# Where the weights lie against the moving tiles: other gaps in SBUF in a two-level Strassen-like short-convolution layer

## The chip, the cores and the metric

The kernel runs on one core of one Trainium2 chip. The metric is device microseconds from launch to end, the median of several runs. The kernel before took 771.57 us (3 runs, 770.79 to 771.90).

## What is computed

With DEPTH = 1 only layer 0 of the reference runs, so the whole computation is one gated short-convolution mixer between two RMS norms, in float32:

```python
u = rms_norm(x, pre_norm)                       # x: 1024 frames x 1024
z, bg, cg, v = split(u @ w_in, 4)               # w_in: 1024 x 8192, four parts of 2048
y = bg * causal_dwconv(cg * v, conv_w) * silu(z)   # 3 taps along the frames
out = x + rms_norm(y @ w_out, post_norm)        # w_out: 2048 x 1024
```

## The kernel before, in words

**Products.** Both matrix products are done in seven products a to g instead of eight (Strassen's scheme in Winograd's form, over halves of the frames and of the contraction). An operand is a sum of blocks, split into a high and a low part in the format fp32r; each product of two blocks is three matmuls, low by high, high by low, high by high. `product` (main stage) issues for one of the 32 pairs of weight rows and one letter 4 x 3 matmuls of 128 by 128 weights with 512 moving columns. For most of the chunks, the products b, f and g are in turn done in seven products a' to g' (`deep_product`): 2 x 3 matmuls each with 256 moving columns. b is done so in 14 chunks, f in 13 and g in 12; elsewhere b, f and g are 512 columns wide like a, c, d, e. The output stage has `out_mm` (512 columns, letters a, c, e, d, g) and `small_mm` (256 columns, for b and f).

**Operands in SBUF.** In the main stage the *moving* operand is a tile U of one letter (`u_a` to `u_g`, 16 KB in each partition) or a second-level sum of parts of it (`ub..`, `uf..`, `ug.._deep`, 2 KB each, in the pool `tmp`). The *weights* lie in pages of 2 KB (`wah`, `wal`, `dwb0h` ...). The weight load of the next matmul runs while the present matmul streams its columns. In the output stage both operands of a product lie in the seven slots that held the U tiles: `ou_*`, `oB*`, `ox_*` move, `oy_*`, `oA*`, `ox_*` are weights. Every slice that a matmul takes begins a multiple of 512 bytes behind its tile's start, so that the distance from the moving operand to the weights, modulo 512, is the same for all matmuls of one pair of tiles. This text calls it **d**: address of the weights less address of the moving operand, modulo 512.

**What sets the addresses.** SBUF pools are laid one behind another in the order in which they are opened. `Shelves` opens one pool for each group of slots in `U_LAYOUT` (the first number names the slots, the second the bytes left free behind the group, by `gap`); `U_SLOTS` says in which slot each tile comes to lie (a: 5, b: 4, c: 2, e: 6, d: 1, f: 3, and g: 0 after the input tile `xb`). Then come 32 pages, then the gap `room_tmp`, then the head's tiles (`xa`, gone after the head) and in their place the pool `tmp` with the second-level sums.

```python
for n, (slots, room) in enumerate(U_LAYOUT):
    pool = ctx.enter_context(tc.tile_pool(name=f"up{n}", bufs=1))
    self.at.update({s: pool for s in slots})
    gap(ctx, tc, f"room{n}", room)
```

The tiles that the pools give out have these places, modulo 512:

| tiles | before |
|---|---|
| U of b, f, g (slots 4, 3, 0) | 64 |
| U of a, c, d, e (slots 5, 2, 1, 6) | 128 |
| pages (all weights of the main stage, all loads) | 128 |
| second-level sums | 64 |
| `xa`, later `gpad` and `acc` | 32 |

So d is 0 for a, c, d and e, and 64 for b, f, g and the second level. In the output stage d is 0, 64 or 448 (that is, -64), by the slots of the two operands.

**Order of the work.** A planner (`Plan`) records the program, sorts each engine's instructions by due times from the table `PLAN`, and emits them. All matmuls come in the order in which they were recorded.

Of the kernel before, what the change touches and what calls it, by code (L numbers as in the profile page):

```python
# [199 lines left out]
class Op:  # L200
# [2 lines left out]


U_LAYOUT = (
    ((0,3,4,), 64),
    ((1,2,5,6,), 0),
)
U_SLOTS = (5, 4, 2, 6, 1, 3, 0, 0, 5, 2, 6, 4, 1, 3, 0, 5, 2, 6, 4, 1, 6, 3, 0, 4, 2, 5, 6, 1, 0, 3, 2, 4, 5, 6, 0, 4, 1, 5, 3, 6, 0, 2)
# [2 lines left out]
def gap(ctx, tc, name, size):  # L212

    if size:
        ctx.enter_context(tc.tile_pool(name=name, bufs=1)).tile([128, size // 4], F32, tag=name, name=name)
# [426 lines left out]
def kernel(  # L642
# [365 lines left out]

    mixed = ExitStack()
    head = ExitStack()  # L1010
    gap(ctx, tc, "room_tmp", 416)
    hp = plan.pool(head.enter_context(tc.tile_pool(name="head", bufs=1, reuse_waits="tile")), 1)

    xa = hp.tile([P, TH, D], F32, tag="xa", name="xa")
# [1079 lines left out]
```

## Time and profile before

| | |
|---|---|
| median of 3 runs | 771.57 us |
| the profiled execution's own time | 771.06 us |
| its span, first to last instruction | 769.3 us |
| TensorE (PE) | 759.3 us busy, 4320 matmuls |
| weight loads (PEld) | 666.1 us, 4320 |
| VectorE (DVE) | 679.9 us |
| ScalarE (ACT) | 459.1 us |
| GpSimd (POOL) | 464.3 us |
| granted clock of TensorE | 0.998 |

The profiled execution's own time is 1.8 us over its span, which is what lies outside the first and last instruction. A matmul's row in the timeline has its start and its modelled length; since matmuls overlap in the pipeline, the time that one costs is read from the start of one row to the start of the next, which this text calls the **pitch**. Rows of the timeline merge neighbours of the same tiles (x2, x24, x96).

### The profile page before, as it was taken

The numbers are of one execution on the slowest core, as the hardware profiler recorded it, in microseconds if no ns is written. First come the engines' busy times: TensorE is split into PE (matmuls) and PEld (weight loads), VectorE is DVE, ScalarE is ACT, GpSimd is POOL, SyncE is SP. The second block draws the span as 40 slices with busy tenths as digits, with TensorE's granted clock in tenths as the row PEclk, the third lists the DMA queues.
The fourth block names the chain that finished last, engine by engine and source line by source line (L and its number), as shares of the span: only waits on it lengthen the run. The fifth ranks groups of instructions, "written<-read, shape, count | busy, mean of one in ns | idle before, by whom it ended". The sixth has DMA issues, their size and how long they took to land.

```text
span 769.3 us, 12814 instructions
## 1 busy us (share of the span) xinstructions
PE 759.3 (99%) x4320; PEld 666.1 (87%) x4320; DVE 679.9 (88%) x1022; ACT 459.1 (60%) x880; POOL 464.3 (60%) x416
## 2 busy tenths in 40 slices
PE   8999999999999999999999999999999999999996
PEld 7888889898989898988898998989888889889885
DVE  6899978999888989999989999799998898877993
ACT  7765678675656565556555665556653656565731
POOL 2509997889675778696789678585639100700421
PEclk9999999999999999999999999999999999999999
DMA  9212425344333547566858484927465998566842
GB/s 316 69 53 71 123 79 150 105 128 141 100 117 97 171 111 198 137 177 174 239 138 240 110 234 107 251 84 217 127 174 177 332 373 289 199 220 205 276 149 109
DMA packets 117137, 130.11 MB, mean 169 GB/s; under 512 B 7320, under 2 KB 74704, under 8 KB 116944
## 3 DMA queue, kind: packets, MB, share of 16 engines
q1 hardware_dynamic: 112560, 120.77, 49.2%
q0 software_dynamic: 4352, 8.39, 7.0%
q8 instruction: 34, 0.56, 0.3%
q14 instruction: 31, 0.25, 0.1%
q10 hardware_dynamic: 160, 0.14, 0.1%
HBM read 101.74 MB, written 44.30 MB: 190 GB/s over the span
## 4 chain that ended last, share of the span: by engine, by line
PE 98%; DVE 1%; DMA 0%; ACT 0%; POOL 0%; issue 0%; POOLq 0%; ACTq 0%
PE px L279 39%; PE pv L279 15%; PE po_x L279 11%; PE px2b L279 5%; PE px2f L279 4%; PE px2g L279 3%; PE pp L279 3%; PE po_v L279 3%; PE pv2b L279 3%; PE pv2f L279 2%; PE pf_x L279 1%; PE pb_x L279 1%; PE py2b L279 1%; PE py L279 1%; PE pv2g L279 1%; PE pb_v L279 1%
## 5 line engine op out<-in xcount | busy, mean ns | idle before, releaser
L279 PE MATMUL px<-u_c,wch 128*128 128x512 f32 x248 | 76.5, 389 | 0.0
L279 PE MATMUL px<-u_a,wah 128*128 128x512 f32 x248 | 76.4, 389 | 0.0
L279 PE MATMUL px<-u_d,wdh 128*128 128x512 f32 x248 | 76.4, 389 | 0.0
L279 PE MATMUL pv<-u_e,weh 128*128 128x512 f32 x248 | 76.4, 389 | 0.0
L279 ACT COPY beside<-raw 128x512 f32<-128x512 f32 x67 | 39.6, 591 | 31.9 <-DVE dwf2l L279 10.5
L279 DVE SCALAR_TENSOR_TENSOR cv<-gpad,cw,cv 128x1024 f32<-128x1024 f32 x32 | 51.7, 1615 | 2.9 <-ACT cv L279 2.6
L279 PEld LDWEIGHTS px<-u_c,wch 128*128 128x128 f32 x248 | 46.6, 188 | 8.8
L279 PEld LDWEIGHTS px<-u_a,wah 128*128 128x128 f32 x248 | 46.5, 188 | 8.7
L279 PEld LDWEIGHTS pv<-u_e,weh 128*128 128x128 f32 x248 | 46.6, 188 | 8.7
L279 PEld LDWEIGHTS px<-u_d,wdh 128*128 128x128 f32 x248 | 46.5, 188 | 8.6
L279 POOL TENSOR_TENSOR sf<-raw,sc 128x512 f32<-128x512 f32 x30 | 46.4, 1545 | 10.1 <-DVE sc L279 5.8
L279 PE MATMUL px<-u_d,wdl 128*128 128x512 f32 x124 | 48.4, 390 | 0.0
L279 PE MATMUL px<-u_a,wal 128*128 128x512 f32 x124 | 48.3, 390 | 0.0
L279 PE MATMUL px<-u_c,wcl 128*128 128x512 f32 x124 | 48.3, 389 | 0.0
L279 PE MATMUL pv<-u_e,wel 128*128 128x512 f32 x124 | 48.2, 389 | 0.0
L279 POOL TENSOR_TENSOR rs_post<-ve_post,minus_half 128x1 f32<-128x1 f32 x7 | 6.5, 942 | 67.6 <-DVE ve_post L279 67.6
L279 POOL TENSOR_TENSOR raw<-raw,raw 128x512 f32<-128x512 f32 x31 | 44.6, 1437 | 3.3 <-DVE se L279 1.9
L279 POOL TENSOR_TENSOR sc<-se,raw 128x512 f32<-128x512 f32 x25 | 35.1, 1404 | 18.5 <-PE px2b L279 7.9
L279 ACT COPY sna<-px 128x512 f32<-128x512 f32 x30 | 17.6, 585 | 45.5 <-PE px L279 45.5
L279 POOL TENSOR_TENSOR se<-raw,raw 128x512 f32<-128x512 f32 x22 | 33.0, 1500 | 16.7 <-DMA raw<-in_sc_w_in 11.1
L279 DVE TENSOR_TENSOR wcl<-sc,wch 128x512 fp32r<-128x512 f32 x31 | 31.6, 1018 | 3.5 <-ACT wch L279 3.5
L279 POOL TENSOR_TENSOR sne<-snc,sne 128x512 f32<-128x512 f32 x12 | 18.4, 1536 | 23.1 <-ACT snc L279 23.1
(486 smaller groups left out, 2643.5 us busy)
## 6 DMA issues: line engine op xcount, KB each, us to landing
raw<-in_sc_w_in SPq DMA_DIRECT2D x128, 256.0 KB, 4.3
y_d<-cv SPq DMA_DIRECT2D x16, 512.0 KB, 2.9
s_d<-s SPq DMA_DIRECT2D x32, 256.0 KB, 4.7
t_d<-in_sc_w_out POOLq DMA_DIRECT2D x16, 512.0 KB, 8.8
tb<-in_sc_w_out SPq DMA_DIRECT2D x16, 256.0 KB, 3.2
t_d<-in_sc_w_out SPq DMA_DIRECT2D x16, 256.0 KB, 4.7
t_d<-t_d SPq DMA_DIRECT2D x16, 256.0 KB, 4.5
s<-y_d SPq DMA_DIRECT2D x16, 256.0 KB, 4.5
```

The lines of the kernel that those rows point to most:

```text
L279: getattr(engine, name)(*(self.plain(a) for a in args), **{k: self.plain(a) for k, a in kw.items()})
```

## The change

It changes free bytes between tiles, and nothing else: the group of slots 0, 3, 4 becomes three groups, with 64, 64 and 96 free bytes behind them, and the gap `room_tmp` shrinks from 416 to 192 bytes.

```diff
 U_LAYOUT = (
-    ((0,3,4,), 64),
+    ((0,), 64),
+    ((3,), 64),
+    ((4,), 96),
     ((1,2,5,6,), 0),
 )
...
-    gap(ctx, tc, "room_tmp", 416)
+    gap(ctx, tc, "room_tmp", 192)
```

Every engine has the same instructions in the same order with the same waits before and after; only the addresses differ. They become, modulo 512:

| tiles | before | after | d before | d after |
|---|---|---|---|---|
| U of b (slot 4) | 64 | 192 | 64 | 96 |
| U of f (slot 3) | 64 | 128 | 64 | 160 |
| U of g (slot 0) | 64 | 64 | 64 | 224 |
| second-level sums | 64 | 0 | 64 | 288 |
| U of a, c, d, e (slots 5, 2, 1, 6) | 128 | 288 | 0 | 0 |
| pages | 128 | 288 | | |
| `xa`, `gpad`, `acc` | 32 | 480 | | |

In the output stage, by weights and moving operand:

| products | matmuls | d before | d after |
|---|---|---|---|
| `oy`,`ou` of a0, c0, e1, d1 | 4 x 48, 512 columns | 0 | 0 |
| c1; d0 | 48; 48 | 0 | 64; 128 |
| a1, e0; g0; g1 | 96; 48; 48 | 448 | 416; 352; 288 |
| `oA1_b`,`oB1_b` | 24, 256 columns | 448 | 288 |
| `ox_b`,`oB2_b`; `oA3_f`,`oB3_f` | 24; 24 | 448 | 416 |
| `oA1_b`,`oB3_b`; `oA3_f`,`oB1_f` | 24; 24 | 0 | 448; 128 |
| `oA3_b`,`oB3_b`; `oA2_f`,`oB2_f`; `ox_f`,`oB2_f` | 3 x 24 | 64 | 160 |
| `oA2_b`,`ox_b` | 24 | 64 | 96 |
| `oA1_f`,`oB1_f` | 24 | 64 | 224 |
| the other four of 256 columns | 4 x 24 | 0 | 0 |

One more thing is different: before, the U tiles, the pages and the second-level sums all begin at a multiple of 64 bytes; after, the U tiles of a, c, d, e and the pages begin 32 bytes past one.

## The prediction

> **What bounds the kernel.** I read the page's first part and its chain first: who is busy all the time, and whose work makes up the chain that ended last.
>
> ```profile
> PE 759.3 (99%) x4320; PEld 666.1 (87%) x4320; DVE 679.9 (88%) x1022; ACT 459.1 (60%) x880; POOL 464.3 (60%) x416
> PE 98%; DVE 1%; DMA 0%; ACT 0%; POOL 0%; issue 0%; POOLq 0%; ACTq 0%
> ```
>
> TensorE is busy for 99% of the span and makes up 98% of the chain. There is next to no wait to take away or to add: the time is the sum of the matmuls' pitches, and a change of addresses can act on it through the pitch alone. So I looked for the pitch by d in the timeline of TensorE, from the start of the first row of a run of matmuls to the start of the next run.
>
> First 512 columns, at d = 0 (`u_c`, 12 matmuls) and at d = 64 (`u_f`, 12 matmuls, starting at 607.17 and ending where `ubgh_deep` begins):
>
> ```profile
> 355.74 0.39 PE L279 MATMUL px<-u_c,wcl 128*128 128x512 f32 x1
> ...
> 358.46 0.28 PE L279 MATMUL px<-uggh_deep,dwg 128*128 128x256 f32 x1
> ...
> 607.17 0.39 PE L279 MATMUL pv<-u_f,wfl 128*128 128x512 f32 x1
> ...
> 609.97 0.28 PE L279 MATMUL px2b<-ubgh_deep,dwb 128*128 128x256 f32 x1
> ```
>
> At d = 0 the twelve take 358.46 - 355.74 = 2.72 us, 226.7 ns each; at d = 64 they take 609.97 - 607.17 = 2.80 us, 233.3 ns each. The granted clock is 0.998 over the whole span (front table), so the clock is not the reason. It isn't an accident of two places either: the groups of all matmuls of a kind show the same in a matmul's length.
>
> ```profile
> L279 PE MATMUL px<-u_c,wch 128*128 128x512 f32 x248 | 76.5, 389 | 0.0
> L279 PE MATMUL px<-u_g,wgh 128*128 128x512 f32 x56 | 17.6, 394 | 0.0
> L279 PE MATMUL pv<-u_f,wfh 128*128 128x512 f32 x40 | 12.5, 394 | 0.0
> L279 PE MATMUL py<-u_b,wbh 128*128 128x512 f32 x24 | 7.5, 394 | 0.0
> L279 PE MATMUL pp<-u_b,wn11h 128*128 128x512 f32 x8 | 2.7, 394 | 0.0
> ```
>
> `u_c` (d = 0) has a mean of 389 ns, `u_g`, `u_f` and `u_b` (d = 64) 394 ns in every group. All three kinds have 128 by 128 weights and 512 columns; what the layout sets apart is d.
>
> Then 256 columns at d = 64 in the main stage, 24 matmuls of `u_b`, `u_f` and two second-level sums in one run up to the next `u_d`:
>
> ```profile
> 379.12 0.28 PE L279 MATMUL pv2b<-u_b,dwb2l 128*128 128x256 f32 x1
> ...
> 381.95 0.39 PE L279 MATMUL px<-u_d,wdl 128*128 128x512 f32 x1
> ```
>
> 381.95 - 379.12 = 2.83 us, 117.9 ns each (117.5 in the twelve rows from 358.46 on); I take **117.7**. The other values of d at 256 columns, and d = 448 at 512, stand in the output stage, where one row merges a whole product:
>
> ```profile
> 613.46 22.05 PE L279 MATMUL po_x<-ou_a,oy_a 128*128 128x512 f32 x96
> 635.34 2.99 PE L279 MATMUL pb_x<-oB_b,oA_b 128*128 128x256 f32 x24
> 638.17 3.03 PE L279 MATMUL pb_y<-oB_b,oA_b 128*128 128x256 f32 x24
> 641.03 2.90 PE L279 MATMUL pb_x<-oB_b,oA_b 128*128 128x256 f32 x24
> 643.77 3.02 PE L279 MATMUL pb_v<-oB_b,oA_b 128*128 128x256 f32 x24
> ...
> 652.32 2.89 PE L279 MATMUL pb_x<-ox_b,oA_b 128*128 128x256 f32 x24
> 655.05 21.95 PE L279 MATMUL po_x<-ou_c,oy_c 128*128 128x512 f32 x96
> 676.83 22.06 PE L279 MATMUL po_v<-ou_e,oy_e 128*128 128x512 f32 x96
> ...
> 698.74 2.99 PE L279 MATMUL pf_x<-oB_f,oA_f 128*128 128x256 f32 x24
> 701.56 2.99 PE L279 MATMUL pf_y<-oB_f,oA_f 128*128 128x256 f32 x24
> ```
>
> A run's time is the next row's start less its own. At d = 448: 638.17 - 635.34 = 2.83, 117.9 ns. At d = 0: 641.03 - 638.17 = 2.86, 119.2 ns. At d = 64 there are two answers: 698.74 to 701.56 is 2.82, **117.5**, but 641.03 to 643.77 is 2.74, 114.2, and 652.32 to 655.05 is 2.73, **113.8**. For 512 columns, `ou_c` (both halves d = 0) takes 676.83 - 655.05 = 21.78 for 96, 226.9 ns; `ou_a` takes 21.88, and with its first half at d = 0 (48 x 0.2269 = 10.89) the second, at d = 448, is left with 10.99, **229.0 ns**.
>
> So the trace has three values of d out of the sixteen multiples of 32. With 512 columns 0 is the best (226.8) and both neighbours are dearer; with 256 columns 0 is the dearest (119.2), and the neighbours cost 117.7 or, in some runs, 114. A matmul's length follows the pitch and names these states:
>
> ```profile
> L279 PE MATMUL pb_y<-oB_b,oA_b 128*128 128x256 f32 x24 | 3.0, 282 | 0.0
> L279 PE MATMUL pb_x<-ox_b,oA_b 128*128 128x256 f32 x24 | 2.9, 276 | 0.0
> L279 PE MATMUL px2b<-u_b,dwb0h x56: 281/281/281, 106.5 to 584.3; 128*128 128x256 f32 x56
> ```
>
> The product at 119.2 has a mean length of 282 ns, the one at 113.8 of 276, and `u_b` in the main stage (the third row: least, median and greatest length, first and last start) 281 from first to last. What it doesn't show is any of the new values 96, 160, 224, 288, 352 and 416.
>
> On this a rule of the Trainium skill speaks against the change. "TensorE: Matmul & The Clock Gate", Part 2, step 1, says that the moving operand and the weight load have two independent SBUF read ports, so that loading the next weights takes no read bandwidth from the running matmul; and "SBUF — State Buffer", section "Who interferes with whom", that TensorE never waits on anyone. By that rule d could not matter; the trace does not agree (226.7 against 233.3 ns above).
>
> **The change part by part.** No instruction, wait or transfer is added, removed or moved past another, so everything is count times pitch.
>
> *The second level, main stage.* The counts come from these groups; a group has 4 matmuls a chunk, which gives 14, 13 and 12 chunks, 39 in all.
>
> ```profile
> L279 PE MATMUL px2b<-u_b,dwb0h 128*128 128x256 f32 x56 | 10.5, 281 | 0.0
> L279 PE MATMUL px2f<-u_f,dwf0h 128*128 128x256 f32 x52 | 9.8, 281 | 0.0
> L279 PE MATMUL px<-u_g,dwg0h 128*128 128x256 f32 x48 | 9.0, 281 | 0.0
> ```
>
> 39 chunks x 7 products x 6 matmuls = 1638 matmuls of 256 columns, all at d = 64 now (336 `u_b`, 312 `u_f`, 288 `u_g`, 702 second-level sums), and at 96, 160, 224 and 288 after. Bounds of a new pitch: 113.8 from below, 119.2 from above, so 1638 x -3.9 = -6.4 us to 1638 x 1.5 = +2.5 us. I take 117.7, no change: it is the main stage's own row at d = 64, and the row at the other side of zero (448) has 117.9; two values of d that are far apart in address agree on it.
>
> *b, f and g of 512 columns.* The groups above hold 56 + 40 + 24 high-weight matmuls; the low weights add half as many, 180 in all, and the first products of `u_b` and `u_f` another 48 (the row of `pp<-u_b` and three like it, 8 high each and half as many low). 228 matmuls, now at 233.3. Bounds: down to 226.7 (-1.5 us); nothing dearer than 233.3 is shown for a steady run, and I let the other end be as far above, +1.5 us, an estimate. I take no change.
>
> *The output stage, 512 columns.* c1 and d0 leave d = 0 for 64 and 128: 96 x (233.3 - 226.7) = +0.6 us, where 64 is a value that the trace has. a1, e0, g0 and g1 leave 448 (229.0) for 416, 352 and 288: 192 matmuls, bounds 226.7 and 233.3, -0.4 to +0.8 us; I take the upper, since with 512 columns every step away from zero costs, and 448 is the one nearest to it: +0.8 us.
>
> *The output stage, 256 columns.* Two products leave d = 0: 48 x (117.7 - 119.2) = -0.1 us. Three of those at d = 64 now run at 114 and leave for 160 and 96; at 117.7 that is 72 x 3.7 = +0.3 us. The rest stays where it is.
>
> *Products that keep d = 0.* 4 x 372 in the main stage (248 + 124, from the `u_c` group) and 4 x 48 in the output stage, 1680 matmuls; their operands move together, now to 32 bytes past a multiple of 64. I take nothing, from tiles that lie so already: `xa` is at 32, `xb` at 64 modulo 512.
>
> ```profile
> L279 PEld LDWEIGHTS pk<-ident,xa x32: 138/140/143, 7.4 to 16.6; 128*128 128x128 f32 x32
> L279 PEld LDWEIGHTS pk<-ident,xb x32: 139/140/143, 26.7 to 38.6; 128*128 128x128 f32 x32
> L279 DVE TENSOR_SCALAR xa<-xa,rs_pre x5: 480/752/753, 6.6 to 11.9; 128x1024 f32<-128x1024 f32 x3, 128x512 f32<-128x512 f32 x2
> L279 DVE TENSOR_SCALAR xb<-xb,rs_second x2: 747/750/753, 24.1 to 24.7; 128x1024 f32<-128x1024 f32 x2
> ```
>
> A weight load from either takes 140 ns, and VectorE 750 to 752 ns. No *moving* operand lies so in the trace, which leaves a case open below. The head's transposes (weights from `xa`, d from 416 to 352) are bound to these loads, and I leave them as they are. "SBUF — State Buffer" in the Trainium skill (the box on cachelines) counts SBUF lines of 16 bytes; all the new addresses are multiples of 32, and by that rule this part costs nothing, as I take it.
>
> **Sum:** 0 + 0 + 0.6 + 0.8 - 0.1 + 0.3 = +1.6 us on the execution's own 771.06, 772.7. The median is 771.57, 0.5 above it, so the median becomes 771.57 + 1.6 = **773.2 us**. It all reaches the end, since TensorE has no gap that could hide it.
>
> **The rivals.** *A, faster: the second level falls into the quick rhythm.* At d = 64 the same matmuls run at 117.7 in one place and at 113.8 in another, steadily each; where the weight load meets the stream at another point, the 1638 may settle at 114. For it: the quick rhythm exists, and 0 is the worst d with 256 columns, so that more distance may be better. Against: in the main stage d = 64 never leaves 281, from 106.5 to 584.3 us. Price -6.4 + 1.6 = -4.8, **766.8 us**; with the 512-column ones at 226.7 too and no loss in the output stage, 771.6 - 6.4 - 1.5 = 763.7. It decides once some 700 of the 1638 (the sums alone) are quick: 702 x -3.9 = -2.7. VectorE would allow it:
>
> ```profile
> 500.00:600.00 100.00, 100.00 (x568) 87.81 (x567) 93.75 (x134) 55.47 (x103) 65.17 (x55) 1.00 0.55 161
> ```
>
> Its 93.75 of 100 us leave 6, and the gain is under 1%.
>
> *B, slower: the second level meets as at d = 0.* If its new places act like 0, 1638 x 1.5 = +2.5, with the rest +4.1: **775.7 us**, more if a place is worse than any shown. For it: three values don't map sixteen. Against: 64 and 448 both avoid it.
>
> *C, slower: a stream that begins 32 bytes past a multiple of 64 costs extra.* Price for 1680 matmuls between the step from 226.8 to 229.0 (2.2 ns, +3.7) and that to 233.3 (6.6 ns, +11.1): 776.9 to 784.3, with the rest; the nearest row gives **776.9**. For it: no moving operand lies so before. Against: loads and VectorE don't care.
>
> *D: the change does nothing,* because d isn't the cause of the rows above: **771.6 us**. Against: the groups at 389 and 394, and the output stage's rows, which differ by slot alone. The rule of the Trainium skill on the two read ports, cited above, would give this time.
>
> **How the numbers follow.** A measurement of this kernel can tell about 0.2%, 1.5 us, from no change. Chances: my forecast 0.36 (its own range 771 to 775, since +0.6 rests on rows and +0.8 on a bound; 0.22 slower, 0.12 within, 0.02 faster), A 0.32 (0.30 faster, 0.02 within), B 0.15, C 0.12, D 0.05. Faster 0.32, within 0.19, slower 0.22 + 0.15 + 0.12 = 0.49. The range takes in A but for its best end and C's lower part: 764.5 to 779; beyond it I leave 0.05 below and 0.09 above.
>
> **What would show it.** In the profile after, the groups of `u_b`, `u_f`, `u_g` and the sums by form give each new d its own pitch: my forecast wants lengths of 281 at 256 columns and 394 at 512. Lengths near 276 in the sums and `u_b` are A, 282 and more are B. `u_c` at 389 denies C, 391 or more shows it. `ou_c` should take 22.1 us for its 96 instead of 21.78. I am wrong if the pitch depends on d in finer steps than the trace shows, and wholly if a group that keeps its d changes.

## The result, and the profile after

| | before | after |
|---|---|---|
| median of 3 runs | 771.57 us (770.79 to 771.90) | 776.75 us (776.65 to 776.80) |
| ratio, 95% interval | | 1.0069 (1.0046 to 1.0092) |
| the profiled execution's span | 769.3 us | 774.9 us |
| granted clock of TensorE | 0.998 | 0.997 |

The change costs 5.2 us, 0.7%, which is slower by more than the 0.2% that can be told here. The prediction had 773.2: slower was its likeliest case, but it took +1.6 where +5.2 came. The page after, busy time of each engine, and its chain by engine:

```profile
PE 765.6 (99%) x4320; PEld 668.5 (86%) x4320; DVE 673.9 (87%) x1022; ACT 458.5 (59%) x880; POOL 461.4 (60%) x416
...
PE 98%; DVE 1%; DMA 0%; ACT 0%; POOL 0%; issue 0%; POOLq 0%; ACTq 0%
```

The shape is as before: TensorE is busy for 99% of the span and is 98% of the chain, with as many matmuls, and its busy time has grown by 765.6 - 759.3 = 6.3 us. (VectorE and GpSimd have become shorter by 6 and 3 us, which nobody waits for.) So the question is which matmuls have a longer pitch. First the output stage after, in rows of the timeline (start, length, and so on as before):

```profile
617.00 22.28 PE L281 MATMUL po_x<-ou_a,oy_a 128*128 128x512 f32 x96
639.12 3.01 PE L281 MATMUL pb_x<-oB_b,oA_b 128*128 128x256 f32 x24
641.96 3.04 PE L281 MATMUL pb_y<-oB_b,oA_b 128*128 128x256 f32 x24
644.84 3.04 PE L281 MATMUL pb_x<-oB_b,oA_b 128*128 128x256 f32 x24
647.72 3.03 PE L281 MATMUL pb_v<-oB_b,oA_b 128*128 128x256 f32 x24
...
656.30 3.01 PE L281 MATMUL pb_x<-ox_b,oA_b 128*128 128x256 f32 x24
659.15 22.26 PE L281 MATMUL po_x<-ou_c,oy_c 128*128 128x512 f32 x96
681.25 22.30 PE L281 MATMUL po_v<-ou_e,oy_e 128*128 128x512 f32 x96
```

`ou_c` takes 681.25 - 659.15 = 22.10 us for its 96 matmuls, the figure that the prediction gave, against 21.78 before. `ou_a` takes 639.12 - 617.00 = 22.12 against 21.88. Of 256 columns, the third row of `pb` (from 644.84: `oA3_b`,`oB3_b`, now at d = 160) takes 647.72 - 644.84 = 2.88 us for its 24, 120.0 ns each, where the same row took 2.74 before; the quick rhythm of 114 ns that it had is gone, and so it is in `ox_b` (659.15 - 656.30 = 2.85, 118.8 ns each, at d = 96).

Then the groups of the main stage after, by form (busy us, mean ns of one, idle before):

```profile
L281 PE MATMUL px<-u_a,wah 128*128 128x512 f32 x248 | 77.1, 392 | 0.0
L281 PE MATMUL pv<-u_e,weh 128*128 128x512 f32 x248 | 77.0, 392 | 0.0
L281 PE MATMUL px<-u_c,wch 128*128 128x512 f32 x248 | 76.8, 391 | 0.0
L281 PE MATMUL px<-u_d,wdh 128*128 128x512 f32 x248 | 76.7, 390 | 0.0
...
L281 PE MATMUL px2b<-u_b,dwb0h 128*128 128x256 f32 x56 | 10.7, 283 | 0.0
L281 PE MATMUL px2f<-u_f,dwf0h 128*128 128x256 f32 x52 | 10.0, 286 | 0.0
L281 PE MATMUL px<-u_g,dwg0h 128*128 128x256 f32 x48 | 9.0, 280 | 0.0
```

The last three are the ones whose d changed: 283, 286 and 280 ns where all had 281. The first four kept d = 0 and were at 389 before (the row of `u_c` in the prediction); now they have 392, 392, 391 and 390. That is the outcome for which the prediction said that it would be wholly wrong.

From all matmul records of the two traces, each pitch (start to next start) summed by class:

| class | matmuls | d before, after | mean pitch before, after (ns) | difference (us) | forecast |
|---|---|---|---|---|---|
| `u_a`, `u_e`, `u_c`, `u_d` | 1536 | 0, 0 | 229.7, 227.3, 227.1, 227.1; 231.7, 229.7, 229.5, 228.1 | 0.78 + 0.92 + 0.87 + 0.36 = **+2.93** | 0 |
| output, 512 columns | 288 | 0 or 448; 64, 128, 288, 352, 416 | 226.9 to 229.4; 233.3 to 233.9 | **+1.47** | +1.4 |
| output, 256 columns | 336 | as in the table of the change | | **+0.53** | +0.2 |
| second level: `u_b` | 336 | 64, 96 | 118.1, 118.8 | +0.23 | 0 |
| second level: `u_f` | 312 | 64, 160 | 118.1, 119.6 | +0.47 | 0 |
| second level: `u_g` | 288 | 64, 224 | 117.8, 117.0 | -0.23 | 0 |
| second level: sums | 702 | 64, 288 | 118.1, 118.2 | +0.08 | 0 |
| `u_b`, `u_f`, `u_g`, 512 columns | 228 | 64; 96, 160, 224 | | +0.15 | 0 |

They add up to 5.63; with the small rest the sum over all records is 5.58, and the span grew by 774.9 - 769.3 = 5.6. More than half of it is in products whose operands lie exactly as far apart as before.

Where inside such a product the time goes is seen in the rows of one run of `u_c` after (a row of one and a row of two make three matmuls):

```profile
374.71 0.39 PE L281 MATMUL px<-u_c,wcl 128*128 128x512 f32 x1
...
375.41 0.40 PE L281 MATMUL px<-u_c,wcl 128*128 128x512 f32 x1
...
376.10 0.39 PE L281 MATMUL px<-u_c,wcl 128*128 128x512 f32 x1
...
376.79 0.39 PE L281 MATMUL px<-u_c,wcl 128*128 128x512 f32 x1
...
377.47 0.28 PE L281 MATMUL px2f<-ufch_deep,dwf1l 128*128 128x256 f32 x1
```

The run of 12 takes 377.47 - 374.71 = 2.76 us, not 2.72; each third of it has 0.70, 0.69, 0.69 and 0.68 us. It starts slow and comes to the old pitch (0.68 for three, 226.7 each) at its end. The single pitches of such runs, as medians by position in the trace, in ns:

```
u_c after u_g at 224: 234 229 231 231 236 228 233 231 226 227 227 226   2759 in all, 12 runs
u_e after sums at 288: 233 236 228 233 231 227 227 226 227 227 226 227   2747, 12 runs
u_e after u_f at 160: 233 233 236 224 231 236 228 233 231 226 227 227   2764, 13 runs
u_e before, after 256 columns at 64: 227 throughout                     2720, 25 runs
```

In the first and the third row the product ahead is six matmuls long, and six sums at 288 stand ahead of it.

### The profile page after: what moved, and what is told of

It is laid out like the page before. It is cut to its first block, busy times and chain, and to the rows that moved or that the text cites. A ratio compares the mean times of both kernels' runs of the same rounds, so it can differ in the third digit from the quotient of the medians.

```text
span 774.9 us, 12814 instructions
## 1 busy us (share of the span) xinstructions
PE 765.6 (99%) x4320; PEld 668.5 (86%) x4320; DVE 673.9 (87%) x1022; ACT 458.5 (59%) x880; POOL 461.4 (60%) x416
## 4 chain that ended last, share of the span: by engine, by line
PE 98%; DVE 1%; DMA 0%; ACT 0%; POOL 0%; issue 0%; POOLq 0%; ACTq 0%
PE px L281 39%; PE pv L281 15%; PE po_x L281 11%; PE px2b L281 5%; PE px2f L281 4%; PE px2g L281 3%; PE pp L281 3%; PE po_v L281 3%; PE pv2b L281 3%; PE pv2f L281 2%; PE pf_x L281 1%; PE pb_x L281 1%; PE py2b L281 1%; PE py L281 1%; PE pv2g L281 1%; PE pb_v L281 1%
## 5 line engine op out<-in xcount | busy, mean ns | idle before, releaser
L281 POOL TENSOR_TENSOR sf<-raw,sc 128x512 f32<-128x512 f32 x30 | 44.8, 1495 | 11.1 <-DVE sc L281 5.9
L281 DVE TENSOR_TENSOR sna<-px2b,sna 128x256 f32<-128x256 f32 x56 | 23.1, 413 | 11.8 <-PE px2b L281 11.8
```

The source lines that it names most:

```text
L281: getattr(engine, name)(*(self.plain(a) for a in args), **{k: self.plain(a) for k, a in kw.items()})
```

## The experiments

**The theories.** *T, carried over:* the matmuls of a run at d = 0 settle at 226.7 ns only after some that are slower, and how many those are is set by the product that ran just before; after second-level matmuls at d = 64 there are none, after the new distances the list of single pitches has 3 to 9 ahead of the first 227. Worked out for `u_e`: 13 runs x 44 ns + 12 x 27 = 0.90 us, of +0.92 measured. Over all four letters, the 103 runs of twelve that stand behind 256 columns take 3.17 us more than 103 x 2720 ns after the change and 0.35 more before it (pauses of single matmuls): 2.82 of the +2.93. *C, the prediction's rival:* a moving operand that begins 32 bytes past a multiple of 64 costs extra. Already against C: in the output stage after, `ou` of a0, c0, e1 and d1 lie so as well, and have 226.9 to 227.6 ns, before 226.9 to 227.5; but the main stage is another place, so it is tried there. *G*, formed later: what matters is whether the neighbours' d is a multiple of 64.

Each experiment's time stands beside the kernel before on the same chip. "Runs" are the runs of 12 matmuls of 512 columns at d = 0, and the ns of one run are the mean over all runs of that letter behind that neighbour.

**Before, all addresses 32 bytes on.** The gap lies ahead of the first U tile; every d stays.

```diff
+    gap(ctx, tc, "room_first", 32)
     up = plan.pool(Shelves(ctx, tc), 7)
```

> Before, with 32 free bytes ahead of the first U tile: every address of U tiles, pages and sums moves by 32, every d stays as before. Theory T (a run of matmuls starts in the rhythm that the run before left behind; a product at d = 0 only locks into its 226.7 ns at once when that rhythm suits): same as before, 771.6 us within 0.8, u_c and u_a at a mean of 389 ns. Rival C (a moving operand that begins 32 bytes past a multiple of 64 costs extra): the products that keep d = 0 pay as they did after the change, +2.9 us or more, 774.5 us and up, u_c at 391.

771.33 us against 771.33, ratio 0.9997 (0.9988 to 1.0007). Its groups by form:

```profile
L279 PE MATMUL px<-u_a,wah 128*128 128x512 f32 x248 | 76.5, 389 | 0.0
L279 PE MATMUL px<-u_c,wch 128*128 128x512 f32 x248 | 76.4, 389 | 0.0
```

389 ns in both, although each tile now begins 32 bytes past a multiple of 64. The 32 bytes alone do nothing: C falls.

**After, with the same gap,** so that the U tiles of a, c, d, e and the pages begin at a multiple of 64 again, and each d is that of the kernel after.

```diff
+    gap(ctx, tc, "room_first", 32)
     up = plan.pool(Shelves(ctx, tc), 7)
```

> After, with 32 free bytes ahead of the first U tile: every d as after the change, but the U tiles of a, c, d, e and the pages begin at a multiple of 64 again. Theory T: as after, 776.7 us within 0.8, means of u_a and u_e 392, of u_c 391. Rival C: the 2.9 us of the products that keep d = 0 come back, 773.8 us, means 389.

777.26 us, ratio 1.0076 (1.0058 to 1.0095). Groups by form:

```profile
L281 PE MATMUL px<-u_a,wah 128*128 128x512 f32 x248 | 77.1, 392 | 0.0
L281 PE MATMUL pv<-u_e,weh 128*128 128x512 f32 x248 | 77.0, 392 | 0.0
```

392 and 392 as in the kernel after: the loss doesn't go with the 32 bytes. With both, only differences of addresses are left as a cause.

**Before, the second-level sums alone at d = 288.**

```diff
-    gap(ctx, tc, "room_tmp", 416)
+    gap(ctx, tc, "room_tmp", 192)
```

> Before, with the gap room_tmp at 192 instead of 416: only the second-level sums move, from d = 64 to 288. Theory T: u_d and u_e, which follow a run of sums in 26 places, pay some 24 to 27 ns a run (as in the profile after), +0.7 us with 0.1 for the sums themselves, 772.3 us; in the profile u_d's and u_e's twelve after sums take 2744 to 2747 ns, while u_a and u_c, which follow u_f, u_g and u_b at d = 64, take 2720. Rival (each matmul pays for its own d alone, and the loss at d = 0 has to do with the pages' or the U tiles' own place): +0.1 us, 771.7 us, and u_d and u_e take 2720.

773.37 us, ratio 1.0025 (1.0016 to 1.0035): more than T had said. The sums themselves give +0.14 us; `u_c` +1.12, `u_e` +0.91, `u_d` +0.20, all three with d = 0 as ever. Groups by form:

```profile
L279 PE MATMUL px<-u_c,wch 128*128 128x512 f32 x248 | 77.3, 393 | 0.0
L279 PE MATMUL pv<-u_e,weh 128*128 128x512 f32 x248 | 77.0, 392 | 0.0
L279 PE MATMUL px<-u_d,wdh 128*128 128x512 f32 x248 | 76.5, 390 | 0.0
L279 PE MATMUL px<-u_a,wah 128*128 128x512 f32 x248 | 76.4, 389 | 0.0
```

And rows of its timeline: a run of `u_d` behind twelve `u_b` matmuls, then twelve `u_f` and a run of `u_a`, then six sums, six `u_b` and a run of `u_c`.

```profile
365.49 0.39 PE L279 MATMUL px<-u_d,wdl 128*128 128x512 f32 x1
...
368.21 0.28 PE L279 MATMUL px2f<-u_f,dwf0l 128*128 128x256 f32 x1
...
369.63 0.39 PE L279 MATMUL px<-u_a,wal 128*128 128x512 f32 x1
...
372.35 0.28 PE L279 MATMUL px2b<-ubch_deep,dwb1l 128*128 128x256 f32 x1
...
373.06 0.28 PE L279 MATMUL pv2b<-u_b,dwb1l 128*128 128x256 f32 x1
...
373.76 0.39 PE L279 MATMUL px<-u_c,wcl 128*128 128x512 f32 x1
...
376.53 0.28 PE L279 MATMUL px2f<-ufch_deep,dwf1l 128*128 128x256 f32 x1
```

`u_d` takes 368.21 - 365.49 = 2.72 us and `u_a` 372.35 - 369.63 = 2.72. `u_c` takes 376.53 - 373.76 = 2.77, though the six matmuls ahead of it (from 373.06) are `u_b` at d = 64; the sums at 288 lie one product further back. This holds for all 24 such runs of `u_c` (2765 ns in the mean) and 13 of `u_e` behind six `u_f` (2765). Where twelve at d = 64 stand just ahead, runs of `u_d` and `u_a` have 2720. In the rows above a run at d = 0 lies between these twelve and the sums, but the 12 runs of `u_a` behind twelve `u_g` that follow twelve sums have 2720 too. T expected `u_c` unharmed, and was too narrow: what is carried over reaches back past six matmuls, and here it was gone after twelve.

**After, the sums alone back at d = 64.**

```diff
-    gap(ctx, tc, "room_tmp", 192)
+    gap(ctx, tc, "room_tmp", 416)
```

> After, with the gap room_tmp back at 416: the second-level sums have d = 64 again, all else is as after the change. Theory T: u_d and u_e lock at once where they follow sums, -0.65 us, and -0.1 for the sums, so 776.0 us; u_a and u_c, which follow u_f and u_g and u_b, stay at 2742 to 2764 ns. Rival (own place): 776.6 us, u_d and u_e unchanged at 2734 to 2764 ns everywhere.

775.24 us, ratio 1.0048 (1.0032 to 1.0064). Groups by form:

```profile
L281 PE MATMUL px<-u_a,wah 128*128 128x512 f32 x248 | 77.1, 392 | 0.0
L281 PE MATMUL px<-u_c,wch 128*128 128x512 f32 x248 | 76.8, 391 | 0.0
L281 PE MATMUL px<-u_d,wdh 128*128 128x512 f32 x248 | 76.7, 390 | 0.0
L281 PE MATMUL pv<-u_e,weh 128*128 128x512 f32 x248 | 76.3, 389 | 0.0
```

`u_e`, half of whose runs stand behind the sums, is at 389 again (2720 ns a run behind the sums, and 2724 behind six `u_f`). `u_a`, behind `u_f` and `u_g`, keeps its 392. One distance was put back, and `u_e` behind it came back, as T has it.

Two things are not as T said. `u_c` behind six `u_b` went up, from 2753 to 2771 ns a run. And `u_d` behind twelve sums takes 2735 in 12 of 13 runs (2744 after the change), not 2720, although the sums have d = 64 again. Rows of one such place, where six `u_b` at 96 and six `u_f` at 160 stand ahead of the twelve sums:

```profile
381.98 0.28 PE L281 MATMUL px2b<-ubdh_deep,dwb2l 128*128 128x256 f32 x1
...
382.46 0.28 PE L281 MATMUL px2b<-ubdl_deep,dwb2h 128*128 128x256 f32 x1
...
383.36 0.39 PE L281 MATMUL px<-u_d,wdl 128*128 128x512 f32 x1
...
386.10 0.28 PE L281 MATMUL px2b<-ubgh_deep,dwb 128*128 128x256 f32 x1
```

The first four sums take 382.46 - 381.98 = 0.48 us, 120 ns each, the other eight 383.36 - 382.46 = 0.90, some 113 each, and `u_d` 386.10 - 383.36 = 2.74. In all 13 such places the single pitches are near 116, 118, 122 and 118 ns, and then 113 or 114. This is the quick rhythm of the output stage, in the main stage; the same kind of sums at the same distance has 117.8 where it follows a run at d = 0. So one distance, 64, has two rhythms, and what ran before chooses between them. The quick one doesn't hand over to a run at d = 0 without loss, and twelve matmuls don't always clear what stood ahead of them. The sums as a whole give -0.74 us against the kernel after, where T had -0.1.

**Before, with d = 192, 128, 32 and 256** for g, f, b and the sums: three multiples of 64, to test G.

```diff
-    ((0,3,4,), 64),
+    ((0,), 64),
+    ((3,), 96),
+    ((4,), 32),
...
-    gap(ctx, tc, "room_tmp", 416)
+    gap(ctx, tc, "room_tmp", 224)
```

> Other distances: d = 192 for g, 128 for f, 32 for b, 256 for the sums; a, c, d, e keep 0. Theory T with hypothesis G (256 columns at a d that is a multiple of 64 leave a rhythm that suits a product at d = 0; odd multiples of 32 don't): u_a, which follows f at 128 or g at 192, and u_e, which follows sums at 256 or f, take 2720 ns a run, while u_c and u_d pay where they follow b at 32; about 774 us. T without G (64 alone suits): nearly every run pays 14 to 44 ns, 776 us or more. The rival that each matmul pays for its own d alone: 2720 everywhere.

776.81 us, ratio 1.0072 (1.0057 to 1.0087). `u_a` behind `u_f` at 128: 2764 ns a run, behind `u_g` at 192: 2757; `u_d` behind sums at 256: 2747, behind `u_b` at 32: 2748. None of the three multiples of 64 spared the run behind it: G falls.

**Before, with d = 448, 384, 320 and 480** for g, f, b and the sums.

```diff
-    ((0,3,4,), 64),
+    ((0,), 64),
+    ((3,), 64),
+    ((4,), 320),
...
-    gap(ctx, tc, "room_tmp", 416)
+    gap(ctx, tc, "room_tmp", 0)
```

> Other distances: d = 448 for g, 384 for f, 320 for b, 480 for the sums. T with G: u_a (after f or g) and u_d after b take 2720 ns a run, u_e and u_d after sums at 480 pay; b, f and g of 512 columns between 229 and 234 ns. T without G: nearly every run pays. About 773 with G, 776 or more without.

773.91 us, ratio 1.0036 (1.0022 to 1.0049). `u_d` behind twelve `u_b` at 320 takes 2720 ns (14 runs), behind sums at 480 it takes 2766. 320 is the first new value that spares the run behind it. The second level is quicker than before at two others: `u_g` at 448 has 115.6 ns, the sums at 480 have 117.1. The 115.6 is a mean of two rhythms, as the groups by form show:

```profile
L281 PE MATMUL px<-u_g,dwg2h 128*128 128x256 f32 x48 | 9.0, 281 | 0.0
...
L281 PE MATMUL px<-u_g,dwg0h 128*128 128x256 f32 x48 | 8.8, 276 | 0.0
```

The second belongs to the twelve `u_g` that follow twelve sums: 113.3 ns each from the first to the last, in all 12 places. The first stands behind a run of `u_a` and has 118.3. `u_a` pays behind both `u_f` and `u_g`, as without G; the kernel stays below 776 with the help of the quick `u_g` (-0.62 us) and of the sums (-0.72).

**Before, with d = 416, 352, 0 and 128** for g, f, b and the sums.

```diff
-    ((0,3,4,), 64),
+    ((0,), 64),
+    ((3,), 352),
+    ((4,), 0),
...
-    gap(ctx, tc, "room_tmp", 416)
+    gap(ctx, tc, "room_tmp", 352)
```

> Other distances: d = 416 for g, 352 for f, 0 for b, 128 for the sums. T with G: u_a after f or g pays 20 to 45 ns a run, u_d after b at 0 and after sums at 128 takes 2720. b runs at 120 ns with 256 columns (d = 0 in the output stage before: 119.2) and at 226.7 with 512. About 775 us. T without G: u_d pays too.

776.88 us, ratio 1.0076 (1.0059 to 1.0093). `u_d` behind `u_b` at d = 0, its own distance, still takes 2747 ns, so being alike doesn't help. `u_a` behind `u_f` at 352 takes 2734, behind `u_g` at 416 it takes 2764. All second-level pitches are 118.3 (352) to 119.8 (416).

**Before, with all four at 448,** which had the lowest pitch off zero with 512 columns.

```diff
-    ((0,3,4,), 64),
+    ((0,3,4,), 448),
...
-    gap(ctx, tc, "room_tmp", 416)
+    gap(ctx, tc, "room_tmp", 32)
```

> One distance for b, f, g and the sums as in the kernel before, but 448 instead of 64. From the output stage before: 117.8 ns with 256 columns and 229 with 512, so 228 x 4.3 = -1.0 us in the main stage; in the output stage four products go from 448 to 64, +0.8 us. T with G: the products at d = 0 take 2720 ns a run, and the kernel 771 to 772 us. T without G: they pay 20 to 40 ns a run, 773 to 775 us.

774.80 us, ratio 1.0047 (1.0032 to 1.0062). Here b, f and g of 512 columns win 0.73 us (`u_g` 229.7 for 233.3 ns), the second level is the same (117.9 to 118.1), but `u_a`, `u_c`, `u_d` and `u_e` lose 0.99 + 0.99 + 0.85 + 0.90 = 3.73: every run behind 256 columns takes 2756 to 2758 ns. The output stage adds 0.9. In the main stage, with the second level left at its pitch, this is the carry-over by itself, and it decides.

**Before, with all four at 320, at 352, at 480.** One value for b, f, g and the sums each time, `room_tmp` being 160, 128 and 0:

```diff
-    ((0,3,4,), 64),
+    ((0,3,4,), 320),
...
-    gap(ctx, tc, "room_tmp", 416)
+    gap(ctx, tc, "room_tmp", 160)
```

> One distance for b, f, g and the sums, 320. T: in the run with 448, 384, 320 and 480 the twelve of u_d after twelve of b at 320 took 2720 ns, as after 64, and 2765 after six; so after a run of twelve at 320 the products at d = 0 should lock, and 320 is the one value but 64 that may keep pace with before: 771.5 to 773 us, u_a, u_c, u_d, u_e at 2720 to 2735 ns a run. If only the d of the run before counted and 64 alone suits: 774 to 777.

771.15 us against 771.21, ratio 0.9996 (0.9986 to 1.0005). Its group of `u_c`, by form:

```profile
L279 PE MATMUL px<-u_c,wch 128*128 128x512 f32 x248 | 76.4, 389 | 0.0
```

The single pitches of runs behind 256 columns are 227 throughout, the second level has 117.7 to 117.8: 320 is like 64 in everything. The U tiles of a, c, d, e begin at 384 modulo 512 here and at 128 before, so the place itself does nothing. (In its profiled execution `u_g` of 512 columns shows 248.0 ns, 1.24 us in all, with an idle time behind VectorE in its row; that is a wait, not a pitch.)

> One distance, 352. T: u_a after f at 352 took 2734 ns, u_e 2719 after sums at 128 and six of f; so 10 to 15 ns a run are lost, +1.3 us, and 256 columns at 352 cost 117.4 to 118.3 (no change): 772.5 to 774.5 us with the output stage. A fixed price for each d without a memory gives no ground for less than the 774 to 777 of the other layouts.

775.24 us, ratio 1.0048 (1.0033 to 1.0063), above what was expected. Runs take 2730 to 2737 ns (+1.1 us), the second level is dearer (118.6 to 119.1 ns: +1.4), the output stage +0.9 with 512 columns (+0.8 of it where 448 became 160) and +0.5 with 256, and `u_g` of 512 columns +0.6, in pauses of single matmuls (372 and 498 ns instead of 233) in the same run of `u_g` that pauses with 320. The expectation had the runs nearly right (+1.3), but took the second level to be unchanged.

> One distance, 480. T: the sums at 480 took 117.1 ns in a mixed layout, and left 2744 to 2766 ns behind; so 256 columns gain up to 1 us and the products at d = 0 lose 24 to 45 ns a run, 2.5 to 4.5 us: 773 to 776 us.

773.13 us, ratio 1.0026 (1.0016 to 1.0036), as expected. Groups by form:

```profile
L279 PE MATMUL px2b<-u_b,dwb0h 128*128 128x256 f32 x56 | 10.4, 279 | 0.0
...
L279 PE MATMUL px<-u_a,wah 128*128 128x512 f32 x248 | 76.8, 391 | 0.0
```

The second level is quicker, 279 ns long and 116.8 to 117.2 from start to start, -1.54 us in all; the runs behind 256 columns take 2744 or 2745 ns, apart from pauses of single matmuls, and the four letters lose 2.66. A gain where it was looked for is more than paid back by products that were not touched.

**Before, with a, c, d, e at d = 256 and b, f, g and the sums at 320.**

```diff
-    ((1,2,5,6,), 0),
+    ((1,2,5,6,), 256),
...
-    gap(ctx, tc, "room_tmp", 416)
+    gap(ctx, tc, "room_tmp", 160)
```

> Before, with 256 free bytes between the U tiles of a, c, d, e and the pages (and room_tmp at 160): d = 256 for a, c, d, e and 320 for b, f, g and the sums; the output stage keeps its distances. If d counts modulo 256 only, this is the same as before, 771.3 us, with means of 389 ns for u_a, u_c, u_d, u_e and 281 for 256 columns. If it counts modulo 512, the 1536 matmuls of a, c, d, e run at 229 to 234 ns as at every other distance shown but 0, +3.5 to +11 us, 775 to 782 us.

771.13 us against 771.47, ratio 0.9997 (0.9988 to 1.0006). Groups by form:

```profile
L279 PE MATMUL px<-u_c,wch 128*128 128x512 f32 x248 | 76.4, 389 | 0.0
L279 PE MATMUL px<-u_a,wah 128*128 128x512 f32 x248 | 76.4, 389 | 0.0
```

Every d of the main stage is 256 more than before, and the pitches there are the same within 0.2 ns: 227.0 for `u_c` (227.1 before), 118.1 for the sums (118.1). d counts modulo 256, not 512. No layout here is faster than the kernel before, and those that equal it are the ones that have its distances modulo 256.

## Why the prediction was right and wrong

- **"Everything is count times pitch"** held: the sum of the pitches, 5.58 us, is the growth of the span, and no wait took part in it.
- **Output stage, 512 columns: right.** c1 and d0 gave 0.31 + 0.29 = +0.60 (said +0.6), a1, e0, g0 and g1 together +0.87 (said +0.8). For 288, 352 and 416 the dear bound was the true one: 233.3 to 233.9 ns. That was in part luck, since the reason for taking it, that 448 is cheap for being nearest to zero, doesn't hold: 64 is as near to zero as 448 (-64), and has 233.3 ns where 448 has 229.0.
- **Output stage, 256 columns: the size was off,** +0.53 for +0.2. d = 160 and 416 have 119.8 to 120.2 ns, dearer than the 119.2 of d = 0, and five products went there, where 117.7 was taken.
- **Second level: inside its bounds.** +0.55 us for 0, out of -6.4 to +2.5. The four new distances have four pitches, 117.0 to 119.6 ns, so that "two values that agree" didn't stand for the others; they happened to cancel in part. Rival A, the quick rhythm, didn't occur with the new distances, but it does exist in the main stage: twelve `u_g` at 448 had 113.3 ns in one layout and 117.8 in another, and eight of twelve sums at 64 had 113 behind `u_f` at 160. B came true for `u_f`, and by half for `u_b`; the sums, the largest group, kept their pitch.
- **b, f and g of 512 columns:** +0.15 for 0, inside its bounds.
- **The failed step: "Products that keep d = 0 ... I take nothing."** Those of the main stage cost +2.93 us, more than any other term, 0.78 + 0.92 + 0.87 + 0.36. The only price that the prediction had for them was rival C's, 3.7 us at least for the 32 bytes. C's total of 776.9 lies near the result, but C is denied by two runs: 32 bytes without new distances cost nothing (ratio 0.9997), new distances without the 32 bytes cost the same (1.0076). Its test, "`u_c` at 389 denies C, 391 or more shows it", could not tell C from T. What stands in its place is that a product's pitch depends on the products ahead of it too: 2.82 of the 2.93 us are in the 103 runs behind 256 columns.
- **The time: slower, as was likeliest, but outside the forecast's own range** of 771 to 775. The wide range, 764.5 to 779, holds it because C's lower part was let in, and C is denied; that was luck.
- **D, no effect:** denied: the layouts above, all with the same instructions, range from 771.1 to 777.3 us. What the prediction drew from the rule on two independent read ports ("TensorE: Matmul & The Clock Gate" in the Trainium skill, Part 2, step 1), that the distance of the weights can't matter, doesn't hold here. Whether the ports themselves are to blame, no run shows.

That carry-over stood in the trace of before, and in the prediction's own rows. It found "two answers" at d = 64 with 256 columns and kept them as a chance for rival A, without asking what stood ahead. The product from 698.74, at 117.5 ns, follows 512 columns at d = 0; the two at 114, from 641.03 and 652.32, follow 256 columns at d = 0 and at 448. One distance, other neighbours, another pitch.

The same holds with 512 columns. The prediction read the pitch of `u_c` in a run behind 256 columns; there are places where a run at d = 0 follows 512 columns at d = 64. Rows of the timeline of before, a run of `u_c` behind twelve `u_g`, then one of `u_e` behind it:

```profile
597.58 0.39 PE L279 MATMUL px<-u_c,wcl 128*128 128x512 f32 x1
...
598.27 0.40 PE L279 MATMUL px<-u_c,wcl 128*128 128x512 f32 x1
...
598.96 0.39 PE L279 MATMUL px<-u_c,wcl 128*128 128x512 f32 x1
...
599.64 0.39 PE L279 MATMUL px<-u_c,wcl 128*128 128x512 f32 x1
...
600.32 0.39 PE L279 MATMUL pv<-u_e,wel 128*128 128x512 f32 x1
...
603.04 0.28 PE L279 MATMUL pv2b<-u_b,dwb2l 128*128 128x256 f32 x1
```

`u_c` takes 600.32 - 597.58 = 2.74 us, with 0.69 in each of its first two thirds and 0.68 in the others; `u_e`, behind a run of the same d, takes 603.04 - 600.32 = 2.72. Twenty nanoseconds more, at one letter and one d, by the neighbour alone: had the prediction compared runs by what precedes them, it would have had a price for new neighbours, and a term of its own. With these 20 ns for each of the 26 + 24 + 28 + 25 = 103 runs of twelve that stand behind 256 columns, the term would have been +2.1 us, an estimate from the trace of before.

## What to carry to other kernels

Where TensorE is the bound, back-to-back matmuls have a rhythm that the layout sets, and it is carried from one product into the next; an edit of one product's addresses is to be priced at its neighbours too. Compare the same product behind different neighbours in the trace of before, not the mean of its group alone, before taking "its operands keep their distance" for nothing. And a padding that makes one product quicker (480 here, -1.54 us) has to be weighed with what it does to the run behind it (+2.66).

## What the runs showed of the hardware

- **The distance counts modulo 256 bytes.** Pairs 256 apart have the same pitch with 256 columns behind like neighbours: 117.7 and 117.7 ns at 64 and 320, 118.8 and 118.8 at 96 and 352, 117.0 and 117.1 at 224 and 480, 120.0 and 120.2 at 160 and 416 (the last pair in the output stage).
- **A run at d = 0 reaches its pitch on one path.** Nearly all lists of single pitches, whatever the neighbour, end alike: ... 233 236 224 231 236 228 233 231 227 227; the neighbour sets how far up the list the run begins. Behind twelve matmuls of 256 columns only 64 and 320, of the distances tried, let it begin at the end, and 64 only in the rhythm of 117.8 ns (elsewhere it was met once, `u_e` behind six `u_f` at 352 that follow sums at 128: 2719 ns). Six matmuls at 64 didn't undo the sums at 288, and twelve did; but twelve sums at 64 didn't undo six `u_f` at 160 (2735 ns).
- **With 256 columns one distance can have two steady rhythms.** 64 has 117.8 ns behind runs at d = 0, and 113 to 114 in the output stage of before and behind `u_f` at 160; 448 has 117.8 and 113.3. The product ahead decides which.
- **Open:** what in the chip makes the pitch depend on the distance, why 64 and 320 hand over without loss in one of their rhythms, and by what rule the product ahead chooses the rhythm. No run here looks inside a weight load; a quarrel of the weight load with the running stream is an argument and not shown.
